# One layer of a hybrid diffusion backbone on one core: the first norm's modulation steps in one sequence, full-tile rotary parts, an early start on an operand

## The chip, the cores and the metric

The kernel runs on one core of one Trainium2 chip. A core has five engines, each with a queue of its own that it works through in order: TensorE (PE in the profile; its weight loads PEld), VectorE (DVE), ScalarE (ACT), GpSimd (POOL) and SyncE (SP), which here only issues DMAs. An instruction waits at the head of its queue until what it needs is there, and everything behind it waits too. The metric is the device time of one execution in microseconds (us).

## The reference

One layer is applied to 128 context tokens and 512 latent tokens, 640 in all, of width 2048. Context and latent tokens have conditioning vectors of their own.

```python
shift1, scale1, gate1, shift2, scale2, gate2 = split(silu(cond) @ w_ada + b_ada, 6)   # w_ada 2048 x 12288
h = rms_norm(x, g1) * (1 + scale1) + shift1
qkv, z, a, b, q_a, kv_a, k_pe = split(h @ w_in)
gdn_o = gated_deltanet(conv(qkv), z, a, b)              # 8 heads, both directions
q = rms_norm(q_a) @ w_q_b;  k, v = expand(rms_norm(kv_a) @ w_kv_b)
mla_o = softmax(([q_nope, rope(q_rope)] @ [k_nope, rope(k_pe)].T) * 192 ** -0.5) @ v   # 8 heads, rotary width 64
x = x + gate1 * (concat(gdn_o, mla_o) @ w_out)
h2 = rms_norm(x, g2) * (1 + scale2) + shift2
x = x + gate2 * conv_ffn(h2);  y = rms_norm(x, gf)
```

All is fp32. The kernel makes an fp32 product from three products of a faster format: a high part (a cast, on ACT) and a low part (operand minus high part, mostly on VectorE) of each operand, hi x hi + hi x lo + lo x hi.

## The kernel before

Tokens lie along the free axis: an operand tile is 128 features x 640 tokens, and a dense matmul covers 320 tokens. `dense` makes two output tiles (a pair) over four groups of four k-tiles (`kg`); `w_next` splits a weight chunk of 512 KB into its parts (`split_chunk`, lines 129 and 131) and loads further chunks ahead. A list scheduler of the framework fixes each engine's order from the program, so instructions of neighbouring steps interleave; which order results is seen in the program itself.

**First stage.** x is loaded in eight DMAs; ACT squares the sixteen k-tiles, VectorE adds them (line 381), and two fp32 matmuls with a matrix of ones give the column sums (line 244). A *modulation step* `ada(n, ...)` computes 256 columns of the modulation: four raw chunks of `w_ada` (`araw`, three buffers), each split (three buffers for the parts), 32 matmuls with four stationary columns (lines 264 and 265), a copy, and a closing product (line 272, four records in the trace). `part(j)`, for j = 0 to 7, does step j of scale1, makes the two modulated k-tiles (`modulated`: `h_hi` on ACT, `h_lo` on VectorE for even, on GpSimd for odd tiles, line 290), and the first three output tiles (z0 to z2) take them up. Then `dense` makes z3 and z4, with six modulation steps for shift1 (`NSP = 6`) put between its k-groups. The remaining four tiles of shift1 come from the *filler*, `gemv_fill`: VectorE multiplies raw rows of `w_ada` by the conditioning and adds up (lines 324 and 326, two instructions in each step of the filler), and a finish on TensorE (line 309, 16 small fp32 matmuls) closes a job of 16 steps. The shift's own product with `w_in` enters as two more columns (640 and 641) of `h`; z0 to z4 ran without them and get theirs by the filler later.

**Middle stage.** The other columns of `w_in`, with eight DeltaNet heads beside them; the filler goes on with gate1, shift2 and scale2.

**Attention.** 24 steps (8 heads x 3), each with scores, softmax, transposes and the product with v, and the projections of the next head pair in between. A score group is five products (line 1083); the rotary low part `qrl` has 64 rows, the other operands 128. `krs` holds the rotary key's high part in rows 0 to 63 and its low part in rows 64 to 127, `qrs` the query's high part twice. The filler ticks four times in each step by `FM = 0.25`.

**Output projection.** Eight pairs. `m_split(kg)` loads and splits the 16 operand tiles from `mix_d` in the first pair; the sinks add the residual (line 1195) and sum the squares (lines 1202 and 1203); the filler runs at one step for each tick, and what is left of it runs after the last pair. Then come the column sums (line 244) and the second norm.

Of the kernel before, what the change touches and what calls it, by code (L numbers as in the profile page):

```python
# [41 lines left out]
FM = 0.25  # L42
# [3 lines left out]
NSP = 6  # L46
LA = 1
# [3 lines left out]
PK = ()  # L51
SH = 1.0
# [15 lines left out]
def step_kernel(ctx: ExitStack, tc: tile.TileContext, a, dbg=None, stop=None):  # L68
# [183 lines left out]
    def ada_load(c, kg, pl):  # L252
        raw = pl.tile([P, 4, 256], F32, tag="wraw", name="araw", bufs=3)
        sp.dma_start(raw, a["w_ada"][c, kg])
        return raw

    def ada(n, t0, cond, pl):

        ps = bank("ada_ps")
        for kg in range(4):  # L260
            hi, lo = split_chunk(ada_load(n, kg, pl), 256, pl, 3, (4 * n + kg) % 8 in PK)
            for k in range(4):
                kt = kg * 4 + k
                pe.matmul(ps[0:4, 0:256], cond[:, kt, :], hi[:, k, :], start=kt == 0, stop=False)
                pe.matmul(ps[0:4, 0:256], cond[:, kt, :], lo[:, k, :], start=False, stop=kt == 15)
# [3 lines left out]
        def last():  # L269
            ps2 = bank("ada_ps2")  # L270
            for j in range(2):
                pe.matmul(ps2[:, 2 * j:2 * j + 2], m4[:, j * P:(j + 1) * P], con[0:4, K_COMB:K_COMB + 2],
                          start=True, stop=True)
            dve.tensor_tensor(mod[:, t0:t0 + 2, :], ps2[:, 0:4].rearrange("p (j c) -> p j c", c=2),
                              v1(V_BADA + t0, 2).unsqueeze(2).broadcast_to([P, 2, 2]), ALU.add)
# [7 lines left out]

    def modulated(x, rb, hi, lo, kt, scale, v):

        for cc, sl in ((0, slice(0, TL)), (1, slice(TL, T))):
            dve.scalar_tensor_tensor(v[:, sl], x[:, kt, sl], mod[:, scale + kt, cc:cc + 1], rb[:, sl],
                                     ALU.mult, ALU.mult)
        act.copy(hi[:, kt, 0:T], v)  # L289
        (pool if kt % 2 else dve).tensor_tensor(lo[:, kt, 0:T], v, hi.bitcast(F32)[:, kt, 0:T], ALU.subtract)  # L290
# [68 lines left out]
    h_hi = hp.tile([P, KT, T + 2], F32R, name="h_hi")  # L359
    h_lo = hp.tile([P, KT, T + 2], F32R, name="h_lo")  # L360
    zb = hp.tile([P, EZ, 2], F32, name="zb")

    def hmov(kt):
        return h_hi[:, kt, :], h_lo[:, kt, :]

    fill["ps"] = lambda: bank("ada_ps")
    with tc.tile_pool(name="xp", bufs=1, side="right") as xp:
        cond = xp.tile([P, KT, 4], F32R, name="cond")
        dve.tensor_copy(cond[:, :, 0:2], csil)
        dve.tensor_tensor(cond[:, :, 2:4], csil, cond.bitcast(F32)[:, :, 0:2], ALU.subtract)  # L370
        xs = xp.tile([P, KT, T], F32, name="xs")
        for c in range(8):
            sp.dma_start(xs[:, 2 * c:2 * c + 2, :], a["x"][:, 2 * c:2 * c + 2, :])
        acc = xp.tile([P, T], F32, name="acc1")
        for kt in range(KT):
            if kt == 0:
                act.activation(acc, xs[:, 0, :], AF.Square)
            else:
                sq = xp.tile([P, T], F32, tag="sq", name="sq", bufs=2)
                act.activation(sq, xs[:, kt, :], AF.Square)  # L380
                dve.tensor_tensor(acc, acc, sq, ALU.add)
        rb = xp.tile([P, T], F32, name="rb1")
        rstd_bcast(rb, col_sums(acc), 1.0 / D)

        def part(j):
            if j < 8:
                ada(j, 16 + 2 * j, cond, xp)()
                gain(16 + 2 * j, V_N1 + 2 * j, 2)
                for kt in (2 * j, 2 * j + 1):
                    v = xp.tile([P, T], F32, tag="sq", name="v", bufs=2)  # L390
                    modulated(xs, rb, h_hi, h_lo, kt, 16, v)

        def early(i, ps):

            zr = xp.tile([P, T], F32, tag="sq", name="zr", bufs=2)
# [1546 lines left out]
```

## Time and profile before

| | |
|---|---|
| median of 3 runs | 3266.69 us (3266.14 to 3268.99) |
| profiled execution | 3265.16 us, its span 3263.4 us |
| mean granted TensorE clock | 0.968 |
| TensorE, VectorE, ACT, GpSimd busy | 94%, 82%, 45%, 10% of the span |
| DMA | 403.92 MB, mean 124 GB/s |

Busy time of TensorE counts overlapping matmuls from the first start to the last end, so the distance of starts tells more of a matmul's price than its own duration. The granted clock is the share of 2.4 GHz that TensorE got; half is the lower of its two levels.

### The profile page before, as it was taken

The page shows a single profiled execution, that of the slowest core. Times are in us where ns is not written, and L with a number is a line of the kernel's source. Part 1 is how long each engine was busy: PE and PEld are TensorE (multiplying, and loading weights), DVE is VectorE, ACT ScalarE, POOL GpSimd, SP SyncE. Part 2 cuts the span into 40 slices and gives each one's busy share as a digit, 9 for nine tenths or more (in the row PEclk, how much of TensorE's full clock was granted, in tenths as well). Part 3 has the DMA queues.
Part 4 walks back from the last instruction along what each step waited for, and adds up shares of the span by engine and source line. Part 5 has one row for each costly group of instructions (what it writes and reads, how often), then busy time and mean ns, then how long its engine had stood idle before and what let it go on. Part 6 is the DMA issues. An engine that isn't in the chain of part 4 may idle for free. (4 is left out here: it accounts for less than half of the span.)

```text
span 3263.4 us, 54513 instructions
## 1 busy us (share of the span) xinstructions
PE 3071.6 (94%) x21243; PEld 2972.8 (91%) x21243; DVE 2684.3 (82%) x4701; ACT 1453.0 (45%) x2245; POOL 334.3 (10%) x279
## 2 busy tenths in 40 slices
PE   5899999999998998997899999999999989999996
PEld 4689999999998998997899999999999989999995
DVE  7666666767567677998998898898898898999998
ACT  5434555555446543114544444444444454444433
POOL 1201000000000000003200000000010041111111
PEclk9899999999899999998999999999999999999998
DMA  7663222323224126883343333343343332333333
GB/s 271 201 198 86 72 78 67 117 68 100 74 87 135 45 81 236 270 263 121 127 136 97 110 128 108 111 131 110 98 140 102 95 125 94 113 98 110 110 116 121
DMA packets 181474, 403.92 MB, mean 124 GB/s; under 512 B 39392, under 2 KB 57952, under 8 KB 181216
## 3 DMA queue, kind: packets, MB, share of 16 engines
q1 hardware_dynamic: 181216, 400.44, 38.3%
q8 instruction: 167, 2.74, 0.4%
q14 instruction: 91, 0.75, 0.1%
HBM read 361.83 MB, written 38.54 MB: 123 GB/s over the span
## 5 line engine op out<-in xcount | busy, mean ns | idle before, releaser
L922 ACT CAST whi<-wraw 128x1024 fp32r<-128x1024 f32 x256 | 268.8, 1050 | 489.4 <-PE dn L198 202.8
L198 PE MATMUL mm<-b_hi,whi 128*128 128x320 f32 x1344 | 398.6, 310 | 4.2 <-ACT whi L922 3.9
L198 PE MATMUL mm<-b_lo,whi 128*128 128x320 f32 x1344 | 397.8, 310 | 0.0
L923 DVE TENSOR_TENSOR wlo<-wraw,whi 128x1024 fp32r<-128x1024 f32 x256 | 318.0, 1242 | 71.9 <-PE dn L207 62.9
L326 DVE SCALAR_TENSOR_TENSOR aacc<-araw,csil,aacc 128x512 f32<-128x512 f32 x510 | 369.0, 762 | 9.1 <-DMA araw<-in_w_ada_dram 8.7
L198 PE MATMUL mm<-h_lo,whi 128*128 128x320 f32 (+1 forms) x1312 | 318.7, 321 | 17.5 <-POOL h_lo L290 17.5
L198 PE MATMUL mm<-h_hi,whi 128*128 128x320 f32 (+1 forms) x1312 | 324.2, 327 | 7.5 <-ACT h_hi L289 4.8
L198 PE MATMUL dn<-b_hi,whi 128*128 128x320 f32 x1008 | 297.7, 309 | 0.0
L198 PE MATMUL dn<-b_lo,whi 128*128 128x320 f32 x1008 | 297.7, 309 | 0.0
L129 ACT CAST whi<-wraw 128x1024 fp32r<-128x1024 f32 (+1 forms) x138 | 143.0, 1036 | 327.3 <-PE mm L198 227.1
L198 PEld LDWEIGHTS mm<-b_hi,whi 128*128 128x128 f32 x1344 | 253.2, 188 | 5.0 <-ACT whi L922 4.4
L198 PEld LDWEIGHTS mm<-b_lo,whi 128*128 128x128 f32 x1344 | 253.2, 188 | 0.0
L198 PEld LDWEIGHTS mm<-h_lo,whi 128*128 128x128 f32 x1312 | 227.3, 194 | 21.5 <-POOL h_lo L290 19.6
L198 PEld LDWEIGHTS mm<-h_hi,whi 128*128 128x128 f32 x1312 | 227.2, 195 | 13.0 <-ACT h_hi L289 6.8
L1593 PE MATMUL mm<-b_hi,whi 128*128 128x320 f32 x672 | 204.6, 318 | 33.1 <-DVE x_lo L1600 9.4
L207 PE MATMUL mm<-h_hi,wlo 128*128 128x320 f32 (+1 forms) x1312 | 234.1, 318 | 0.0
L922 ACT CAST whi<-us 128x1024 fp32r<-128x1024 f32 (+1 forms) x126 | 123.4, 980 | 230.7 <-PE mm L198 160.3
L207 PE MATMUL mm<-b_hi,wlo 128*128 128x320 f32 x1344 | 224.4, 309 | 0.0
L131 DVE TENSOR_TENSOR wlo<-wraw,whi 128x1024 fp32r<-128x1024 f32 (+1 forms) x138 | 168.2, 1219 | 54.2 <-ACT whi L129 23.7
L207 PEld LDWEIGHTS mm<-h_hi,wlo 128*128 128x128 f32 x1312 | 202.8, 192 | 1.6
L207 PEld LDWEIGHTS mm<-b_hi,wlo 128*128 128x128 f32 x1344 | 204.0, 188 | 0.0
L1593 PE MATMUL mm<-b_lo,whi 128*128 128x320 f32 x672 | 202.2, 314 | 0.0
(534 smaller groups left out, 7461.2 us busy)
## 6 DMA issues: line engine op xcount, KB each, us to landing
wraw<-in_w_up_dram SPq DMA_DIRECT2D x176, 512.0 KB
araw<-in_w_ada_dram SPq DMA_DIRECT2D x272, 256.0 KB
wraw<-in_w_down_dram SPq DMA_DIRECT2D x88, 512.0 KB
wraw<-in_w_in_dram SPq DMA_DIRECT2D x80, 512.0 KB
araw<-in_w_ada_dram SPq DMA_DIRECT2D x56, 512.0 KB
wraw<-in_w_out_dram SPq DMA_DIRECT2D x32, 512.0 KB
graw<-g_d SPq DMA_DIRECT2D x44, 320.0 KB
g_d<-cg SPq DMA_DIRECT2D x44, 256.0 KB
```

What stands on the lines that cost most here:

```text
L129: act.copy(hi[:, :, 0:n], raw[:, :, 0:n])
L131: (pool if on_pool else dve).tensor_tensor(lo[:, :, 0:n], raw[:, :, 0:n], hi.bitcast(F32)[:, :, 0:n], ALU.subtract)
L198: pe.matmul(o, wts[0][:, k, col:col + P], m[:, sl], start=start and k + n == 0, stop=False)
L207: pe.matmul(o, wts[1][:, k, col:col + P], mov(k)[0][:, sl], start=False, stop=stop and k == 3)
L326: dve.scalar_tensor_tensor(acc[:, c, 0:w], raw, vecs[:, kt, c:c + 1], acc[:, c, 0:w], ALU.mult, ALU.add)
L922: act.copy(dst_hi, src)
L923: dve.tensor_tensor(dst_lo, src, dst_hi.bitcast(F32), ALU.subtract)
L1593: pe.matmul(dq[q], wt(w[0], k), bs[(2 * n + k) % 6][m][:, q, :], start=n == grp[0] and k + m == 0, stop=False)
```

## The change

In the first stage:
- All 16 modulation steps (eight of scale1, eight of shift1, `NSP = 8`) run one after the other through `ada_next`; the closing product of a step and what hangs on it (`ada_last`) come after the next step's matmuls. The filler no longer runs here.
- There are eight raw buffers (`AR`) and five for each part (`AH`). In steps 0 to 7 the first of the four chunks isn't split: it goes into fp32 matmuls with an fp32 stationary operand (`condf`, whose columns 2 and 3 are zero).
- The squares of odd k-tiles go to TensorE (two fp32 matmuls each, of 320 columns), those of even ones are added on VectorE as before.
- x and `h` are eight tiles of two k-tiles, and a tile of `h_hi` takes the place of the x tile that it was made from. Both low parts of a step are on VectorE.

In attention and after it:
- `qrl` has 128 rows: ACT copies rows 0 to 63 into rows 64 to 127, and the product goes with the whole of `krs`.
- `FM` is 0.5: the filler gets twice as many ticks.
- In steps 19 to 22 the first four operand tiles of the output projection are loaded and split (`m_early`) into the room of `qn`, whose pool now lasts to the end of the projection.
- `neg` (minus the decay) is made for each head as `cc[:, 3]`.

```diff
-FM = 0.25
+FM = 0.5
-NSP = 6
+NSP = 8
+AR = 8
+AH = 5
     def ada(n, t0, cond, pl):
         ps = bank("ada_ps")
         for kg in range(4):
-            hi, lo = split_chunk(ada_load(n, kg, pl), 256, pl, 3, (4 * n + kg) % 8 in PK)
+            raw = pl.tile([P, 4, 256], F32, tag="wraw", name="araw", bufs=AR)
+            sp.dma_start(raw, a["w_ada"][n, kg])
+            whole = n < 8 and kg == 0
+            movs = ((1, raw),) if whole else [(0, w) for w in split_chunk(raw, 256, pl, AH)]
             for k in range(4):
                 kt = kg * 4 + k
-                pe.matmul(ps[0:4, 0:256], cond[:, kt, :], hi[:, k, :], start=kt == 0, stop=False)
-                pe.matmul(ps[0:4, 0:256], cond[:, kt, :], lo[:, k, :], start=False, stop=kt == 15)
+                for m, (c, w) in enumerate(movs):
+                    pe.matmul(ps[0:4, 0:256], cond[c][:, kt, :], w[:, k, :], start=kt + m == 0,
+                              stop=kt == 15 and m == 1)
...
-        (pool if kt % 2 else dve).tensor_tensor(lo[:, kt, 0:T], v, hi.bitcast(F32)[:, kt, 0:T], ALU.subtract)
...
         for kt in range(KT):
...
+            sq = acc if kt == 0 else xp.tile([P, T], F32, tag="sq", name="sq", bufs=4)
+            act.activation(sq, xs[kt // 2][:, kt % 2, 0:T], AF.Square)
+            if kt % 2:
+                for o, sl in tok_chunks(sums):
+                    pe.matmul(o, ones, sq[:, sl], start=kt == 1, stop=False)
+            elif kt:
                 dve.tensor_tensor(acc, acc, sq, ALU.add)
+        for o, sl in tok_chunks(sums):
+            pe.matmul(o, ones, acc[:, sl], start=False, stop=True)
...
+                    for k, v in enumerate(vs_):
+                        act.copy(h_hi[n][:, k, 0:T], v)
+                        dve.tensor_tensor(h_lo[n][:, k, 0:T], v, h_hi[n].bitcast(F32)[:, k, 0:T], ALU.subtract)
...
+        def ada_next(count):
+            for _ in range(count):
+                n = nada[0]
+                nada[0] += 1
+                f = ada(n, 16 + 2 * n if n < 8 else 2 * n - 16, (cond, condf), xp)
+                ada_last()
+                last.append((n, f))
...
         for kg in range(4):
-            for j in range(LA) if kg == 0 else ():
-                part(j)
-            for j in (2 * kg, 2 * kg + 1):
-                part(j + LA)
+            if kg == 0:
+                ada_next(1)
+                w_load(0)
+                w_load(1)
+            ada_next(3 if kg == 0 else 2)
...
-            ql = mp.tile([64, T], F32R, name="qrl", bufs=5)
+            ql = mp.tile([P, T], F32R, name="qrl", bufs=5)
...
-            dve.tensor_tensor(ql, rr[s, :], st_.bitcast(F32)[s, :], ALU.subtract)
+            dve.tensor_tensor(ql[0:64, :], rr[s, :], st_.bitcast(F32)[s, :], ALU.subtract)
+            act.copy(ql[64:128, :], ql.bitcast(F32)[0:64, :])
...
-                                    (qrl[:, qs], krs[0:64, :]))):
+                                    (qrl[:, qs], krs))):
...
+    def m_early(k):
+        if k == 0:
+            m_first.extend(qp.tile([P, 4, T], F32R, tag=f"qn_{q}", name=f"mf_{q}") for q in ("hi", "lo"))
+        raw = mp.tile([P, T], F32, tag="m0", name="m0", bufs=2)
+        sp.dma_start(raw, mix_d[k])
+        split(m_first[0][:, k, :], m_first[1][:, k, :], raw)
...
     for n, (h, x) in enumerate(steps):
+        if n in (19, 20, 21, 22):
+            m_early(n - 19)
```

SP's queue at the start of the program, from the first modulation weight on, before (`wraw` is a chunk of `w_in`, line 302 a row of the filler):

```order
L254 DMA araw<-in_w_ada_dram 128x1024 x3
L125 DMA wraw<-in_w_in_dram 128x1024
L254 DMA araw<-in_w_ada_dram 128x1024 x3
L125 DMA wraw<-in_w_in_dram 128x4x128
L125 DMA wraw<-in_w_in_dram 128x1024
L254 DMA araw<-in_w_ada_dram 128x1024 x3
L125 DMA wraw<-in_w_in_dram 128x4x128
L302 DMA araw<-in_w_ada_dram 128x512
L254 DMA araw<-in_w_ada_dram 128x1024 x3
```

and after:

```order
L257 DMA araw<-in_w_ada_dram 128x1024 x4
L125 DMA wraw<-in_w_in_dram 128x1024
L125 DMA wraw<-in_w_in_dram 128x4x128
L257 DMA araw<-in_w_ada_dram 128x1024 x12
L125 DMA wraw<-in_w_in_dram 128x1024
L125 DMA wraw<-in_w_in_dram 128x4x128
L257 DMA araw<-in_w_ada_dram 128x1024 x7
L125 DMA wraw<-in_w_in_dram 128x1024
L257 DMA araw<-in_w_ada_dram 128x1024
```

Sixteen raw chunks stand ahead of the second pair of `w_in` chunks, without a filler load among them, where three chunks stood ahead of the first.

VectorE at the start, from its sums of squares on, before (`wlo` are low parts of weights, `v` the modulated tile, `h_lo` its low part):

```order
L381 TENSOR_TENSOR acc_108<-acc_108,sq 128x640 x15
L131 TENSOR_TENSOR wlo<-araw,whi 128x1024 x3
L131 TENSOR_TENSOR wlo<-wraw,whi 128x1024
L131 TENSOR_TENSOR wlo<-araw,whi 128x1024 x3
L274 TENSOR_TENSOR mod<-ada_ps_223,vec 128x4
L131 TENSOR_TENSOR wlo<-wraw,whi 128x4x128
L282 SCALAR_TENSOR_TENSOR mod<-mod,vec 128x4
L287 SCALAR_TENSOR_TENSOR v<-xs,mod,rb_155 128x512
L287 SCALAR_TENSOR_TENSOR v<-xs,mod,rb_155 128x128
L287 SCALAR_TENSOR_TENSOR v<-xs,mod,rb_155 128x512
L287 SCALAR_TENSOR_TENSOR v<-xs,mod,rb_155 128x128
L131 TENSOR_TENSOR wlo<-araw,whi 128x1024
```

and after:

```order
L378 TENSOR_TENSOR acc_116<-acc_116,sq 128x640 x7
L131 TENSOR_TENSOR wlo<-araw,whi 128x1024 x3
L131 TENSOR_TENSOR wlo<-wraw,whi 128x1024
L131 TENSOR_TENSOR wlo<-wraw,whi 128x4x128
L273 TENSOR_TENSOR mod<-ada_ps,vec 128x4
L131 TENSOR_TENSOR wlo<-araw,whi 128x1024
L281 SCALAR_TENSOR_TENSOR mod<-mod,vec 128x4
L396 SCALAR_TENSOR_TENSOR v<-xs_90,mod,rb_174 128x512
L131 TENSOR_TENSOR wlo<-araw,whi 128x1024
L396 SCALAR_TENSOR_TENSOR v<-xs_90,mod,rb_174 128x128
L131 TENSOR_TENSOR wlo<-araw,whi 128x1024
L396 SCALAR_TENSOR_TENSOR v<-xs_90,mod,rb_174 128x512
```

Seven additions stand where fifteen stood, and the low parts of the second step's weights now lie between the parts of the first modulated tile.

VectorE at the end of the output projection, before (`aacc` is the filler, `xt` the residual in a sink, `acc` the sum of squares, `x2t` the second norm's operand):

```order
L326 SCALAR_TENSOR_TENSOR aacc<-araw,csil,aacc 128x512 x4
L1195 SCALAR_TENSOR_TENSOR xt<-pj,mod,xt 128x512
L1195 SCALAR_TENSOR_TENSOR xt<-pj,mod,xt 128x128
L326 SCALAR_TENSOR_TENSOR aacc<-araw,csil,aacc 128x512 x2
L1203 TENSOR_TENSOR acc_12702<-acc_12702,sq_15211 128x640
L326 SCALAR_TENSOR_TENSOR aacc<-araw,csil,aacc 128x512 x2
L1195 SCALAR_TENSOR_TENSOR xt<-mm_14949,mod,xt 128x512
L1195 SCALAR_TENSOR_TENSOR xt<-mm_14949,mod,xt 128x128
L326 SCALAR_TENSOR_TENSOR aacc<-araw,csil,aacc 128x512 x2
L1203 TENSOR_TENSOR acc_12702<-acc_12702,sq_15245 128x640
L326 SCALAR_TENSOR_TENSOR aacc<-araw,csil,aacc 128x512 x2
L131 TENSOR_TENSOR wlo<-wraw,whi 128x1024
```

and after:

```order
L337 TENSOR_TENSOR mod<-ada_ps,vec 128x8
L131 TENSOR_TENSOR wlo<-wraw,whi 128x1024
L281 SCALAR_TENSOR_TENSOR mod<-mod,vec 128x8
L131 TENSOR_TENSOR wlo<-wraw,whi 128x1024
L1222 SCALAR_TENSOR_TENSOR xt<-pj,mod,xt 128x512
L1222 SCALAR_TENSOR_TENSOR xt<-pj,mod,xt 128x128
L1230 TENSOR_TENSOR acc_12845<-acc_12845,sq_15274 128x640
L1222 SCALAR_TENSOR_TENSOR xt<-mm_15063,mod,xt 128x512
L1222 SCALAR_TENSOR_TENSOR xt<-mm_15063,mod,xt 128x128
L131 TENSOR_TENSOR wlo<-wraw,whi 128x1024
L1230 TENSOR_TENSOR acc_12845<-acc_12845,sq_15304 128x640
L1354 TENSOR_TENSOR x2t<-x2t,rb_15343 128x640 x4
```

The filler's rows no longer stand between and behind the last two sinks; its last output (`mod`) lies ahead of them.

## Rows read from the trace of the kernel before

**Rows 1.** Page, line 1: busy us, share and instructions of each engine.
```profile
PE 3071.6 (94%) x21243; PEld 2972.8 (91%) x21243; DVE 2684.3 (82%) x4701; ACT 1453.0 (45%) x2245; POOL 334.3 (10%) x279
```

**Rows 2.** Busy us by window; columns as the windows view prints them.
```profile
25.00:150.00 125.00, 97.91 (x604) 77.83 (x604) 95.20 (x125) 61.16 (x75) 30.97 (x8) 0.89 0.66 214
150.00:206.00 56.00, 54.03 (x399) 45.02 (x396) 35.56 (x39) 28.41 (x33) 0.00 (x0) 1.00 0.70 233
```

**Rows 3.** Waits of the first stage: us in total, times, longest.
```profile
ACT whi L129 <- DMA araw<-in_w_ada_dram: 25.7, 20, 2.5
PE mm L198 <- POOL h_lo L290: 17.5, 7, 4.3
```

**Rows 4.** Tile h_lo, who writes it: duration ns, least, median, most.
```profile
L290 POOL TENSOR_TENSOR h_lo<-v,h_hi x8: 1944/3907/6162, 39.2 to 136.2; 128x640 fp32r<-128x640 f32 x8
L290 DVE TENSOR_TENSOR h_lo<-v,h_hi x8: 814/818/821, 39.4 to 135.3; 128x640 fp32r<-128x640 f32 x8
```

**Rows 5.** Tile z_d, the stores into it: first and last start.
```profile
L397 SPq DMA_DIRECT2D z_d<-zr x5: 320/327/327, 143.4 to 205.7; - x5
```

**Rows 6.** Busy us by window in attention; last, the filler on VectorE.
```profile
1140.00:1180.00 40.00, 39.88 (x286) 37.30 (x285) 36.08 (x69) 16.72 (x37) 0.00 (x0) 1.00 0.42 127
1180.00:1243.00 63.00, 59.19 (x398) 51.19 (x396) 37.72 (x90) 28.52 (x69) 0.00 (x0) 1.00 0.09 33
...
1040.00:1243.00 203.00, 19.89 (x28) 1.00 0.18 58
```

**Rows 7.** Timeline around 1250: start, us, instruction, idle time before it.
```profile
1250.33 1.17 PE L198 MATMUL mm<-m_hi,whi 128*128 128x320 f32 x3 [7.93 <-ACT m_hi L922]
...
1255.88 0.59 PE L198 MATMUL mm<-m_hi,whi 128*128 128x320 f32 x2
...
1249.55 3.08 ACT L922 CAST m_hi<-m 128x640 fp32r<-128x640 f32 x4 [6.86 <-DMA m<-mix_d]
```

**Rows 8.** Timeline after the output projection: PE, then DVE and ACT.
```profile
1503.47 1.40 PE L244 MATMUL mm<-acc,con 128*128 128x320 f32 x2 [9.88 <-DVE acc L1203]
1504.67 3.41 PE L309 MATMUL ada_ps<-con,aacc 128*128 128x1 f32 x16
...
1500.28 0.99 DVE L1195 SCALAR_TENSOR_TENSOR xt<-mm,mod,xt 128x512 f32<-128x512 f32 x2
...
1501.30 0.74 ACT L1202 ACTIVATE sq<-xt 128x640 f32<-128x640 f32 x1 [3.56 <-DVE xt L1195]
```

**Rows 9.** Timeline of PE in the first stage, and tile qs_ps.
```profile
148.49 0.28 PE L264 MATMUL ada_ps<-whi,cond 128*4 128x256 f32 x1
...
151.12 0.28 PE L265 MATMUL ada_ps<-wlo,cond 128*4 128x256 f32 x1
...
154.02 0.60 PE L272 MATMUL ada_ps<-con,m 4*128 4x2 f32 x4
...
172.23 2.52 PE L207 MATMUL mm<-h_hi,wlo 128*128 128x320 f32 x16
174.58 0.28 PE L264 MATMUL ada_ps<-whi,cond 128*4 128x256 f32 x1
...
24.00 2.50 PE L244 MATMUL mm<-acc,con 128*128 128x320 f32 x4 [24.00 <-DVE acc L381]
...
L739 PE MATMUL qs_ps<-Sh,kq x64: 379/380/484, 376.7 to 979.4; 128*128 128x256 f32 x64
```

**Rows 10.** Busy us by window, for the last two columns, DMA.
```profile
180.00:200.00 20.00, 19.27 (x142) 15.71 (x141) 11.48 (x13) 9.32 (x12) 0.00 (x0) 1.00 0.68 221
1260.00:1280.00 20.00, 19.47 (x136) 19.20 (x136) 20.00 (x31) 7.42 (x10) 0.00 (x0) 1.00 0.99 350
```

**Rows 11.** Timeline of PE in a score group and behind it.
```profile
1228.23 0.46 PE L1083 MATMUL mm<-krs,qrs 128*128 128x320 f32 x2
1228.61 0.56 PE L1083 MATMUL mm<-krs,qrl 64*128 64x320 f32 x2
1229.10 0.44 PE L1134 MATMUL pt_ps<-con,pr 128*128 128x128 f32 x2
```

More of the change, by code (lines that the diff above doesn't have):

```diff
@@ L357, in step_kernel @@
     hp = hst.enter_context(tc.tile_pool(name="hp", bufs=1))
-    h_hi = hp.tile([P, KT, T + 2], F32R, name="h_hi")
-    h_lo = hp.tile([P, KT, T + 2], F32R, name="h_lo")
+    xs = [hp.tile([P, 2, HW], F32, name=f"xs{j}", tag=f"h_hi{j}") for j in range(8)]
+    h_hi, h_lo = [], []
     zb = hp.tile([P, EZ, 2], F32, name="zb")
     def hmov(kt):
-        return h_hi[:, kt, :], h_lo[:, kt, :]
+        return h_hi[kt // 2][:, kt % 2, :], h_lo[kt // 2][:, kt % 2, :]
     fill["ps"] = lambda: bank("ada_ps")
@@ L374, in step_kernel @@
         acc = xp.tile([P, T], F32, name="acc1")
+        sums = ps_pair(0)
         for kt in range(KT):
[L376 to L380, printed above, removed]
+            sq = acc if kt == 0 else xp.tile([P, T], F32, tag="sq", name="sq", bufs=4)
[4 more added lines that the diff above has]
+            elif kt:
@@ L381, in step_kernel @@
                 dve.tensor_tensor(acc, acc, sq, ALU.add)
+        for o, sl in tok_chunks(sums):
+            pe.matmul(o, ones, acc[:, sl], start=False, stop=True)
         rb = xp.tile([P, T], F32, name="rb1")
[L383 to L391, printed above, removed]
+        rstd_bcast(rb, sums[:, C0:C0 + T], 1.0 / D)
@@ new lines, in step_kernel, with ada_last @@
+        nada, last = [0], []
+        def ada_last():
+            if last:
+                n, f = last.pop()
+                f()
+                if n < 8:
+                    gain(16 + 2 * n, V_N1 + 2 * n, 2)
+                    vs_ = [xp.tile([P, T], F32, tag="sq", name="v", bufs=4) for _ in range(2)]
+                    for k, v in enumerate(vs_):
+                        for cc, sl in ((0, slice(0, TL)), (1, slice(TL, T))):
+                            dve.scalar_tensor_tensor(v[:, sl], xs[n][:, k, sl], mod[:, 16 + 2 * n + k, cc:cc + 1],
+                                                     rb[:, sl], ALU.mult, ALU.mult)
+                    h_hi.append(hp.tile([P, 2, HW], F32R, name=f"h_hi{n}", tag=f"h_hi{n}"))
+                    h_lo.append(hp.tile([P, 2, HW], F32R, name=f"h_lo{n}"))
+                    for k, v in enumerate(vs_):
+                        act.copy(h_hi[n][:, k, 0:T], v)
+                        dve.tensor_tensor(h_lo[n][:, k, 0:T], v, h_hi[n].bitcast(F32)[:, k, 0:T], ALU.subtract)
+                else:
+                    j, m = n - 8, mod[:, 2 * n - 16:2 * n - 14, :]
+                    act.copy(h_hi[j][:, :, T:T + 2], m)
+                    dve.tensor_tensor(h_lo[j][:, :, T:T + 2], m, h_hi[j].bitcast(F32)[:, :, T:T + 2], ALU.subtract)
@@ L417, in step_kernel @@
         bank_pool[0] = sst.enter_context(tc.tile_pool(name="pss2", bufs=4, space=PSUM))
-        fill["step"] = SH
-        fill["gen"] = gemv_fill([xp, 2, 1], ada_jobs(2 * NSP, 16))
-        todo = list(range(NSP))
-        last = []
         npair = (EZ - 3) // 2
@@ L580, in gdn @@
         dve.reciprocal(rec, ss)
[L581 removed]
+        cc = gp.tile([P, 4, 2, 5], F32, name="cc", bufs=2)
         for d in range(2):
@@ L1243, in o_sink @@
                 x_load(t + 4)
-            dense(lambda kt: (m_hi[:, kt, :], m_lo[:, kt, :]), o_sink, before=m_split if p == 0 else None, alloc=three)
+            dense(lambda kt: tuple(m[:, kt, :] for m in m_first) if kt < 4 else (m_hi[:, kt - 4, :], m_lo[:, kt - 4, :]), o_sink, before=m_split if p == 0 else None, alloc=three)
         for _ in fill["gen"]:
@@ L1249, in step_kernel @@
     nst.close()
+    qst.close()
     fst.close()
```

68 lines of the change are left out of this document (25 added, 43 removed).

## The prediction

> **What bounds the kernel now.** I read the page first: TensorE is busy 94% of the span, VectorE 82%, ACT 45% [rows 1]. So a change pays where it takes instructions from TensorE, where TensorE now waits, or where it runs at the lower of its two clock levels (1.2 instead of 2.4 GHz). Next come the stretches that the change touches. In the first stage (0 to 206 us) TensorE is busy 98 of 125 us between 25 and 150, at a granted clock of 0.89; from 150 on, 54 of 56 at 1.00 [rows 2]. The list of waits of that stage tells what ends last there: ACT waits 20 times for a modulation weight's DMA, 25.7 us in all, and TensorE 17.5 us for GpSimd's low parts of the normed operand [rows 3]. GpSimd takes 3.9 us for such a part where VectorE takes 0.82 [rows 4]. The stage ends with the last z store at 205.7 [rows 5]. In attention TensorE loses nothing between 1140 and 1180 and 4 of 63 us after that [rows 6]. It then stands idle 7.93 us before the output projection [rows 7], and 9.88 us after it, waiting for the sum of squares [rows 8].
>
> **The first stage: work.** Undisturbed, TensorE does a modulation matmul every 0.114 us (24 in a row from 148.49 to 151.12), a dense one every 0.147 us (16 from 172.23 to 174.58), and the four records that close a step in 0.60 us [rows 9]. Before, that is 448 x 0.114 + 480 x 0.147 + 14 x 0.60 = 51 + 71 + 8 = 130 us. From 25.8 to 205 it took 179, so 49 us (38%) went to waits and to the low clock. After, there are 16 steps and no filler on VectorE in this stage. The first quarter of steps 0 to 7 goes in as plain fp32: 32 such matmuls take the place of 64, and as the two new steps bring 64, 448 of the short kind stay. A 4x256 fp32 matmul does not occur before. The nearest row is the 128x256 fp32 product, two records of 0.38 us for each [rows 9]; a record of the short kind lasts 0.28 and comes every 0.114, so I take 0.38 - 0.17 = 0.21 us a record, 0.43 a matmul, 14 us for all. Bounds: 0.114 each (4 us), and 0.73 each (23 us) if they run as the fp32 sums at 24.00 did, two matmuls of 320 columns in 1.83 us, up to the next row at 25.83. With 16 x 0.60 the work is 51 + 71 + 14 + 10 = 146 us, 16 more than before.
>
> **The first stage: start.** The sums of squares move half to TensorE: 18 fp32 matmuls instead of 2. At the 0.92 us of that row they are 16.5 us from about 10 us on, beside ACT's sixteen squares, and end near 26, as before; at half that price ACT ends last, near 20. I count no gain. Then VectorE leads: up to the end of the second step it has six low parts of modulation weights, one and a half of dense weights and most of a modulated tile, some 10 us behind ACT's logarithm, exponential and casts, which end near 28. So the dense matmuls start near 38, when TensorE has done 12 of its 146 us; the other 134 would end at 172.
>
> **The first stage: losses.** What stood behind the two great waits is taken away: eight raw buffers instead of three let weights be asked for ahead, and no low part is left on GpSimd. VectorE, busy 95 of 125 us [rows 2], loses its filler and takes eight more operand parts (6.5 us). The weights are 64 x 0.52 + 5.2 = 39 MB. At the 350 GB/s that a full queue reaches at 1260 they need 111 us, from 17 to 128; at the 221 GB/s of 180 to 200, when three buffers held the queue, 176 us, to 193 [rows 10]. I take a loss of 8% of 134 us, between the 4% of 150 to 206 and the 38% of the whole stage, and get an end near 183: **22 us gained**. Bounds: no loss, 33 gained; 38% lost, 223, so 17 us given away.
>
> **Attention.** A score group's two matmuls on 64 rows take 0.49 us (1228.61 to 1229.10), and the two just ahead of them 0.38, where two of the ordinary dense kind take 0.29 [rows 9, 11]. The excess is 0.28 us, 32 times: 9 us. The Trainium skill, TensorE: Matmul & The Clock Gate, section "Why this matters for your kernels", says that a single matmul on 32 rows takes the time of one on 128; by it the full tile would save 0 and the sum would be 38. Against that, its page TensorEngine Tiling, "Key Properties", says that a change of tiling mode drains the engine, for which this trace has the 0.38 ahead of the group; so I go by the row. I take **8**, since from 1180 on TensorE is not full (59.2 of 63 us [rows 6]); bounds 0 and 13 (half as much again where a transpose stands between the two). The eight copies on ACT are hidden: it is busy 28.5 of the last 63 us; uncovered they would be 6 us.
>
> The filler in attention runs twice as often. Before it has 28 rows there and two openings, 15 steps [rows 6]; the new order has 32 steps. The 17 more, at two rows of 0.7 each, are 23 us of VectorE, besides 3 us for the four early tiles. At 1140 to 1180 VectorE was busy 36 of 40 us and TensorE lost nothing [rows 6]. But about half of the new rows fall in the last two heads, where no projection is left to fill TensorE. I charge **2**; bounds 0 and 11 (each of that half in the way of a softmax).
>
> **Output projection, start.** Its first four operand tiles are there, so the 7.93 us go, and with them the low clock: the first 20 matmuls took 5.55 us (1250.33 to 1255.88) for 20 x 0.147 = 2.9 [rows 7]. That is 10.5. What is late next are tiles 4 to 7: they are asked for at the same point as tiles 0 to 3 before, and cast from 1249.55 on, when the first 48 matmuls (7.1 us from 1242.4) end at 1249.5. About 1 us of wait, and some 2 for tiles 8 to 11, which stand behind six filler loads in SP's queue. **8 gained**; bounds 4 and 10.5.
>
> **Output projection, end.** The filler runs out during the last pair, as the new order shows. Then the last residual (0.99), its square (0.74) and its sum (0.8) follow the last matmul (1493.6) in some 3 us instead of 9.9, and the 3.4 us of closing matmuls leave the space between the two sums [rows 8]. **10 gained**; bounds 7 and 11.
>
> **Sum.** 22 + 8 - 2 + 8 + 10 = 46 us. The profiled execution took 3265.2 us, 1.5 less than the median of the runs shown; 3265.2 - 46 + 1.5 = 3221.
>
> **Rivals.**
> - *The first stage keeps its waits.* In-order queues only find new partners: VectorE for GpSimd, more work on TensorE. For it: 38% lost so far, and VectorE leads the first 38 us. Against: both great waits have a cause that goes. At 38% the stage costs 17 more, so the sum is 7 and the time 3260; at 22% (an end at 202) it gains 3, and the time is 3240.
> - *Attention gives it back.* The filler costs 11 and the full tile brings 0, as the softmax chain sets the pace: 46 - 9 - 8 = 29, 3238. For it: TensorE's 4 us lost from 1180 on. Against: none lost at 1140 to 1180. That 64 rows alone cost nothing would give 3229 (the page's rule above); the 0.49 speaks against it.
> - *The stage goes better.* Nothing lost and the upper ends elsewhere: 33 + 13 + 10.5 + 11 = 67, so 3199.
> - *Slower: the low clock in the first stage.* 64 modulation matmuls with four columns now stand in one row, and TensorE is fed in bursts before 38 us. At the low level 20 dense matmuls took 5.55 us [rows 7], 0.28 instead of 0.147 each, 0.9 us more for each us of work. All of the 134 us would cost 120, and the time 3341. It decides from 59 us on, when 65 of the 134 run low. Against: 24 short ones in a row kept 0.114 [rows 9], and the clock was 1.00 from 150 on.
>
> **How the numbers follow.** The forecast as summed has 0.60 (its own range 3206 to 3234), the first stage at 22% or more lost 0.15, attention giving back 0.08, the rule alone 0.03, the better case 0.08, the low clock 0.06. The range reaches from 3202 to 3248: it leaves out the best and the worst first stage and the low clock, some 0.2. What a measurement of this kernel tells from no change is about 0.2%, 6.5 us; the low clock, and the worst first stage with another loss beside it, are what ends nearer than that or beyond: faster 0.87, same 0.06, slower 0.07.
>
> **What would show it.** The last z store near 183 instead of 205.7, no TensorE wait on GpSimd, ACT's waits for weights well under 25 us; score matmuls of one spacing, 0.29 for each two; the output projection's first matmul within 1 us of attention's last; the sums some 3 us after its last matmul. The forecast is wrong if VectorE or a cast's buffer takes the place of the two waits in the first stage, if the granted clock before 150 stays under 0.9, or if TensorE idles in attention beside filler rows.

## The result and the profile after

The changed kernel takes 3233.65 us (median of four runs, 3224.20 to 3235.11) beside 3267.64 of the kernel before; the ratio is 0.989, 95% interval 0.987 to 0.9909. The profiled execution is the one of 3235.11 us, with a span of 3233.3; it is 30 us shorter than the profiled one of before, and the medians are 34 apart. Forecast were 46 and 3221, with a range of 3202 to 3248. So the sign and the range held, and some 12 us of the gain are missing. Where they are is best read from checkpoints: the start of an instruction that both programs have at the same place (first and last start in the lines of a tile).

| Checkpoint, us | before | changed | ahead by |
|---|---|---|---|
| last z store | 205.7 | 183.4 | 22.3 |
| last mix store of the recurrent heads | 1005.4 | 986.0 | 19.4 |
| first matmul on a rotary low part (scores) | 1040.4 | 1024.4 | 16.0 |
| last matmul on a rotary low part | 1232.7 | 1217.1 | 15.6 |
| last matmul of the output projection | 1493.3 | 1474.2 | 19.1 |
| column sums behind it | 1503.5 | 1477.6 | 25.9 |
| end of the span | 3263.4 | 3233.3 | 30.1 |

The first stage gave what was forecast. Attention, forecast as a gain of 6, lost 3.8 (its start 3.4, the scores 0.4). The output projection gave 3.5 up to its last matmul where 8 were forecast, and 11 behind that (6.8 before the sums, 4.2 after). Some 3 us went in the stretch of the recurrent heads, which the change hardly touches.

The busy line of the page, to be held against [rows 1], shows nothing of this: VectorE and ACT are as busy as before, and GpSimd lost 33 us.

```profile
PE 3075.9 (95%) x21331; PEld 2976.8 (92%) x21331; DVE 2652.0 (82%) x4692; ACT 1457.3 (45%) x2263; POOL 301.7 (9%) x272
```

The windows of the first stage do (for [rows 2]; columns as there): after the first 25 us shown, TensorE is full in every window and its granted clock is 1.00. What is lost now is lost before 50 us.

```profile
25.00:50.00 25.00, 20.11 (x103) 9.79 (x101) 16.23 (x23) 14.46 (x18) 0.00 (x0) 0.80 0.91 322
50.00:75.00 25.00, 25.00 (x168) 18.18 (x167) 20.30 (x31) 13.74 (x19) 0.00 (x0) 1.00 0.65 223
75.00:100.00 25.00, 25.00 (x176) 20.09 (x174) 21.37 (x33) 16.12 (x21) 0.00 (x0) 1.00 0.82 308
100.00:125.00 25.00, 25.00 (x184) 22.59 (x183) 19.77 (x27) 14.73 (x20) 0.00 (x0) 1.00 0.83 294
125.00:150.00 25.00, 25.00 (x195) 20.61 (x195) 18.09 (x22) 17.67 (x24) 0.00 (x0) 1.00 0.90 316
```

The two waits of [rows 3] are gone: in the list of waits of this stage TensorE has none for GpSimd, and ACT's for modulation weights, 25.7 us before, is this line (total, times, longest):

```profile
ACT whi L129 <- DMA araw<-in_w_ada_dram: 1.4, 2, 1.1
```

At the start of attention ACT's timeline shows the new copies (L1033, 0.73 us each) between the casts that were there:

```profile
1003.27 0.73 ACT L1033 CAST qrl<-qrl 64x640 fp32r<-64x640 f32 x1
...
1005.70 0.73 ACT L1033 CAST qrl<-qrl 64x640 fp32r<-64x640 f32 x1
...
1013.79 0.73 ACT L1033 CAST qrl<-qrl 64x640 fp32r<-64x640 f32 x1
1014.52 0.62 ACT L989 COPY sw<-kraw 32x512 f32<-32x512 f32 x1
1015.16 0.73 ACT L1033 CAST qrl<-qrl 64x640 fp32r<-64x640 f32 x1
1015.89 0.62 ACT L990 COPY sw<-kraw 32x512 f32<-32x512 f32 x1
1016.53 0.59 ACT L937 CAST vh<-mm 128x512 fp32r<-128x512 f32 x1
```

Two of them stand ahead of the copies for the rotary key (sw) and of the cast vh. VectorE makes vl from vh, the first score matmul waits for vl, and TensorE comes out of that wait at half speed (score pairs 0.53 us apart, weight-and-value matmuls 0.21 apart instead of 0.12). Its timeline there, the wait in the brackets:

```profile
1017.90 0.90 PE L1099 MATMUL mm<-kh,qh 128*128 128x320 f32 x2 [2.25 <-DVE vl L938]
1018.60 0.73 PE L1099 MATMUL mm<-kl,qh 128*128 128x320 f32 x2
1019.13 0.73 PE L1099 MATMUL mm<-kh,ql 128*128 128x320 f32 x2
1019.67 0.41 PE L1062 MATMUL pj<-whi,kv_hi 128*128 128x256 f32 x1
```

A score group has the spacing that was forecast, to be held against [rows 11]: 0.30 and 0.29 us from each pair to the next.

```profile
1215.12 0.45 PE L1099 MATMUL mm<-krs,qrs 128*128 128x320 f32 x2
1215.42 0.46 PE L1099 MATMUL mm<-krs,qrl 128*128 128x320 f32 x2
1215.71 0.71 PE L1150 MATMUL pt_ps<-con,pr 128*128 128x128 f32 x5
```

The output projection now begins at 1222.78, inside attention's last head, and not 7.93 us after its end [rows 7]. Behind it stand three new waits, and a second spell of half speed after the last of them:

```profile
1222.78 0.54 PE L198 MATMUL mm<-mf_hi,whi 128*128 128x320 f32 x2
...
1237.59 0.86 PE L198 MATMUL mm<-m_hi,whi 128*128 128x320 f32 x4 [2.05 <-ACT m_hi L937]
...
1247.03 0.85 PE L198 MATMUL mm<-m_hi,whi 128*128 128x320 f32 x4 [1.87 <-ACT m_hi L937]
1249.61 0.66 PE L198 MATMUL mm<-m_lo,whi 128*128 128x320 f32 x2 [1.72 <-DVE m_lo L938]
1250.06 0.74 PE L198 MATMUL mm<-m_hi,whi 128*128 128x320 f32 x2
1250.60 1.27 PE L198 MATMUL mm<-m_lo,whi 128*128 128x320 f32 x4
```

The end of the projection came as forecast, 3.06 us of wait where [rows 8] had 9.88, and no closing matmuls of the filler between the two sums:

```profile
1473.17 1.34 PE L207 MATMUL mm<-m_hi,wlo 128*128 128x320 f32 x8
1477.57 1.45 PE L244 MATMUL mm<-acc,con 128*128 128x320 f32 x4 [3.06 <-DVE acc L1230]
```

### The profile page after: what moved, and what is told of

It reads as the page before. It is cut to its first block, busy times and chain, and to the rows that moved or that the text cites. A ratio compares the mean times of both kernels' runs of the same rounds, so it can differ in the third digit from the quotient of the medians.

```text
span 3233.3 us, 54651 instructions
## 1 busy us (share of the span) xinstructions
PE 3075.9 (95%) x21331; PEld 2976.8 (92%) x21331; DVE 2652.0 (82%) x4692; ACT 1457.3 (45%) x2263; POOL 301.7 (9%) x272
## 5 line engine op out<-in xcount | busy, mean ns | idle before, releaser
L317 DVE SCALAR_TENSOR_TENSOR aacc<-araw,csil,aacc 128x512 f32<-128x512 f32 x480 | 342.4, 749 | 12.4 <-DMA araw<-in_w_ada_dram 12.0
```

The source lines that it names most:

```text
L317: dve.scalar_tensor_tensor(acc[:, c, 0:w], raw, vecs[:, kt, c:c + 1], acc[:, c, 0:w], ALU.mult, ALU.add)
```

## The experiments

Single executions of one kernel lie up to 13 us from their median here, so an edit worth 3 us is read from its own stretch of the profile, by the checkpoints above, and the total only bears it out. "Scores" is the stretch between the first and the last matmul on a rotary low part; "start" the one before it, from the recurrent heads' last store; "projection" the one from the last such matmul to the output projection's last matmul. How far these stretches repeat is seen where an edit leaves them alone: in six profiles with the changed kernel's attention the scores took 192.4 to 192.7 us and the start 37.8 to 38.7; in nine profiles with four tiles made ahead the projection took 255.3 to 257.9.

**Filler rate of attention.**

```diff
-FM = 0.5
+FM = 0.25
```

> The changed kernel with the filler of attention back at half its rate (FM 0.25). Theory A, that the doubled filler on VectorE ate what the full rotary tile saved: from the first to the last score matmul some 185 us instead of 193.0, and the steps left over come back at the end of the output projection, where TensorE again waits 7 to 10 us for the sum of squares; in all 3230 to 3236. Rival B, that the softmax chain sets attention's pace and the filler is free there: the scores still take 193 us and only the end is lost, 3240 to 3244.

3242.81 us, 9 more than the changed kernel. The scores took 188.8 us instead of 192.7, so the doubled filler costs 3.9 in attention. But the steps left over come back at the end: TensorE waits 9.75 us for the sum of squares again, and the closing matmuls stand between the sums again.

```profile
1481.49 1.41 PE L244 MATMUL mm<-acc,con 128*128 128x320 f32 x2 [9.75 <-DVE acc L1230]
```

A is half right about the scores (188.8, not 185) and right about the wait at the end; the total is B's. The filler rate is a trade of 4 us in attention for 11 or 12 behind the projection (the table's 11.0, in this run 12.7), and the change makes it well.

**Zeros from GpSimd in place of ACT's copies.** The upper 64 rows of the low part meet the low part of the key; with zeros there the sum is that of the kernel before, on a full tile.

```diff
-            act.copy(ql[64:128, :], ql.bitcast(F32)[0:64, :])
+            pool.memset(ql[64:128, :].bitcast(F32), 0.0)
```

> The changed kernel, but the upper 64 rows of each rotary low part are set to zero by GpSimd instead of copied there by ACT; the product is then that of 64 rows, on a full tile. Theory A, that the four ACT copies at the start of attention (0.73 us each, 2.9 us together) lie on the chain to the first scores: the first score group starts 3 to 4 us sooner against the end of the projection before it, and the whole is 3 to 5 us shorter, 3229 to 3231. Rival B, that ACT's copies are hidden and the start is late for a DMA or for VectorE: no change, 3233.6 within 2. Rival C, that GpSimd's memset is late or in VectorE's way: slower by 1 to 5.

3225.98 us. The start took 36.4 us instead of 38.4 and the scores 188.2 instead of 192.7: 6.5 together. That is A's mechanism, but less at the start than A had (2.0, not 3 to 4) and more in all, for the four copies in the middle of attention count as well. GpSimd, otherwise idle there, makes five of the eight before the first is needed (988.44 to 991.4, VectorE's low part at 998.2):

```profile
988.44 2.92 POOL L1033 MEMSET qrl<- 64x640 f32 x5 [141.44 <-DVE qa L960]
```

**Rotary low parts back on 64 rows**, without copies.

```diff
-            ql = mp.tile([P, T], F32R, name="qrl", bufs=5)
+            ql = mp.tile([64, T], F32R, name="qrl", bufs=5)
...
-                                    (qrl[:, qs], krs))):
+                                    (qrl[:, qs], krs[0:64, :]))):
```

> The changed kernel with the rotary low parts back on 64 rows and without ACT's copies; the rest as changed. Theory A, that a matmul on 64 rows costs 0.28 us a score group on the chip and nothing hides it: from the first to the last score 201 us instead of 193.0, less 3.5 us at the start of attention, 3238 in all. Rival B, that attention from the first score on is paced by the softmax chain and the filler, and the full tile is worth nothing there: the scores take 193 to 195 us, and with the 3.5 us of the start the kernel is 1 to 3 us faster than the changed one, 3231.

3235.38 us, start 35.8, scores 198.3. Against the run with zeros, which differs from this one in the tile and in GpSimd's eight instructions alone, that is 10.1 us of scores: A's mechanism, a little above its price. Against the changed kernel it is 5.6 us of scores, between A and B because ACT's copies went as well, less 2.6 at the start, so 3 in all: the copies eat two thirds of what the tile gives. The rows show the price in the same program, 0.39 us ahead of the group of 64 rows and 0.48 for it:

```profile
1215.62 0.45 PE L1098 MATMUL mm<-krs,qrs 128*128 128x320 f32 x2
1216.01 0.56 PE L1098 MATMUL mm<-krs,qrl 64*128 64x320 f32 x2
1216.49 0.87 PE L1149 MATMUL pt_ps<-con,pr 128*128 128x128 f32 x6
```

**No operand tiles ahead.** The output projection loads and casts all sixteen after attention.

```diff
-        if n in (19, 20, 21, 22):
-            m_early(n - 19)
...
-        m_hi = op.tile([P, 12, T], F32R, name="m_hi")
+        m_hi = op.tile([P, KT, T], F32R, name="m_hi")
```

> The changed kernel without the four operand tiles made ahead: the output projection again loads and casts all sixteen tiles after attention. Theory A, that the tiles made ahead are worth the wait of 7.9 us and the low clock behind it, less the new waits for tiles 4 to 11 (2.05, 1.87 and 1.72 us): slower by 5 to 8, 3239 to 3242. Rival B, that the waits only move to the later tiles and the loads in attention cost as much: within 2 of 3233.6. Rival C, that what ends last in the output projection is VectorE's filler and residuals, so that a late start costs nothing: the column sums start at the same time, 3233.

3243.52 us (3234.66 to 3245.05). The projection stretch took 261.9 us, as before the change (260.6), against 257.1: 4.8 for the four tiles, just below A and far from B and C. Four profiles without tiles made ahead have 260.6 to 262.3, so this is clear of the scatter. Another 2.7 us are scores of 195.4 us, and those go with the clock: between 1075 and 1125 it was 0.90 and 0.93 in this run, where the changed kernel had 0.97 and 1.00 at the same place, with fewer matmul records in the same time.

```profile
1075.50:1100.50 25.00, 24.41 (x164) 23.70 (x163) 21.54 (x45) 11.48 (x25) 0.00 (x0) 0.90 0.35 103
1100.50:1125.50 25.00, 23.25 (x145) 22.74 (x143) 23.39 (x41) 21.38 (x37) 0.00 (x0) 0.93 0.32 103
```

What the tiles cost in attention is better read at the place where their casts and low parts stand, 1154.7 to 1163.4 in the changed kernel. The two score groups around it start at 1149.84 and 1170.22, 20.4 us apart; in the run without tiles the same two start at 1152.79 and 1172.56, 19.8 apart, both at a granted clock of 1.00. So the tiles cost 0.6 us there, and nothing at the start (38.6, against 38.4). First the changed kernel, then the run without tiles:

```profile
1149.80:1170.20 20.40, 19.75 (x135) 19.21 (x134) 11.03 (x22) 9.77 (x18) 0.00 (x0) 1.00 0.17 59
```

```profile
1152.70:1172.50 19.80, 19.56 (x134) 19.05 (x133) 8.15 (x18) 7.12 (x14) 0.00 (x0) 1.00 0.08 28
```

**The first stage alone**: the last three edits undone together (filler rate, 64 rows, no tiles ahead).

```diff
-FM = 0.5
+FM = 0.25
...
-            act.copy(ql[64:128, :], ql.bitcast(F32)[0:64, :])
...
-        if n in (19, 20, 21, 22):
-            m_early(n - 19)
```

> The changed kernel with attention and the output projection as before (filler at its old rate, rotary low parts on 64 rows, no tiles ahead), so that what is new is the first stage with its sixteen steps (and one small VectorE instruction more for each head of the next stage). Theory A, that the first stage alone is worth 22 us and keeps it to the end: last z store between 178 and 184, the scores take 192 us again, TensorE waits 10 us for the sums after the output projection, and the whole gains 20 to 26 us against the kernel before. Rival B, that the middle of the program gives some of it back for a reason that lies in the change: the time from the last z store to the last store of the recurrent heads is 803 or more where the kernel before has 799.7, and the gain is under 19 us.

3248.48 us, ratio 0.9933 (0.9916 to 0.995). Last z store 182.8, start 34.8, scores 192.2, projection 261.7, 10.2 us from its last matmul to the sums: the first stage keeps its 22 us to the end, and attention and projection are those of before. The stretch of the recurrent heads took 804.6, as B has it, but the gain, 20.7 us, is A's.

**No plain fp32 quarters.**

```diff
-            whole = n < 8 and kg == 0
+            whole = False
```

> The changed kernel with every modulation weight split into high and low parts, so without the plain fp32 quarters: 64 short matmuls for 32 fp32 ones. Theory A, that in the first 60 us VectorE leads and the fp32 quarters are there to relieve it: eight low parts more at 1.2 us, of which those of the first steps are on the chain, and the last z store comes 1 to 6 us later. Rival B, that TensorE alone sets the stage: 32 x 0.455 = 14.6 us of fp32 give way to 64 x 0.114 = 7.3, and the last z store comes 7 us sooner.

3225.56 us, last z store at 175.1. In seven profiles of the changed first stage it lies between 178.5 and 183.8, 181.8 in the mean, so B is right: 3 to 9 us gained, where it had 7. The total owes something to luck besides: in this profile (an execution of 3217.41 us) the stretch of the recurrent heads, which the edit leaves alone, took 794.0 us, the shortest of all. VectorE was busier (107.6 us between 25 and 150 instead of 95.8), and TensorE no emptier (120.5 instead of 120.1). The fp32 quarters had cost what was forecast; the changed kernel's timeline has four such matmuls (eight records) in 1.82 us, 0.455 each where 0.43 were taken:

```profile
51.44 1.89 PE L264 MATMUL ada_ps<-araw,condf 128*4 128x256 f32 x8
53.26 0.28 PE L264 MATMUL ada_ps<-whi,cond 128*4 128x256 f32 x1
```

**Which of the two great waits was worth the 22 us?** Four kernels: the changed one with three raw buffers; with the odd low parts of the operand on GpSimd; with both; and the kernel before with its low parts on VectorE.

```diff
-AR = 8
+AR = 3
```

> The changed kernel with three raw buffers for modulation weights instead of eight. Theory A, that ACT's 25.7 us of waiting for these weights had the three buffers for a cause: the wait comes back, and the last z store is 8 to 15 us later than 178 to 184. Rival B, that the weights came late before for the other work of the stage (GpSimd's low parts held the operand, and with it everything behind): the last z store stays within 3 us.

```diff
-                        dve.tensor_tensor(h_lo[n][:, k, 0:T], v, h_hi[n].bitcast(F32)[:, k, 0:T], ALU.subtract)
+                        (pool if k else dve).tensor_tensor(h_lo[n][:, k, 0:T], v, h_hi[n].bitcast(F32)[:, k, 0:T], ALU.subtract)
```

> The changed kernel with the odd low parts of the normed operand back on GpSimd, eight at 3.9 us. Theory A, that they held TensorE: it waits for them again, and the last z store is 8 to 15 us later than 178 to 184. Rival B, that with weights asked for ahead TensorE has other work while GpSimd makes its part, and VectorE, which leads, is relieved of 8 x 0.82 us: within 3 us, or sooner.

> The changed kernel with both causes back in its new order: three raw buffers and the odd low parts on GpSimd. Theory A, that GpSimd's parts cost only where the weights come late: the last z store well behind the 191.3 of three buffers alone, 197 to 205. Rival B, that the order of the steps is what made GpSimd's parts harmless: 190 to 193, and the 12 to 14 us that are still missing to 205.7 belong to the order and to the filler.

And of the kernel before:

```diff
-        (pool if kt % 2 else dve).tensor_tensor(lo[:, kt, 0:T], v, hi.bitcast(F32)[:, kt, 0:T], ALU.subtract)
+        dve.tensor_tensor(lo[:, kt, 0:T], v, hi.bitcast(F32)[:, kt, 0:T], ALU.subtract)
```

> The kernel before with all low parts of the normed operand on VectorE, so that only GpSimd's part in its first stage is undone. Theory A, that TensorE's 17.5 us of waiting for GpSimd were lost time: the last z store comes 8 to 15 us sooner than 205.7. Rival B, that behind that wait stands the one for the weights (three raw buffers), and TensorE only waits for another engine: within 4 us of 205.7.

(The totals of the kernel before and of the changed one are those of the first comparison; beside the edited kernels the kernel before took 3266.82 and 3269.19.)

| First stage | weights | odd low parts | last z store | total, us |
|---|---|---|---|---|
| before | 3 buffers | GpSimd | 205.7 | 3267.64 |
| before, edited | 3 buffers | VectorE | 188.0 | 3250.86 |
| changed | 3 buffers | GpSimd | 196.0 | 3246.24 |
| changed | 3 buffers | VectorE | 191.3 | 3241.86 |
| changed | 8 buffers | GpSimd | 181.2 | 3232.91 |
| changed | 8 buffers | VectorE | 178.5 to 183.8 | 3233.65 |

In the old order the low parts alone are worth 17.7 us. In the new order they are worth 4.7 with three buffers (between A's and B's numbers) and nothing with eight (181.2, where the seven profiles of the changed first stage have 181.8 in the mean). The buffers are worth 8 to 13 us, or 15 with the low parts on GpSimd. So A holds for the three buffers, B for the low parts in the new order, and in the old order A, with more than it had. The two waits are not two terms of a sum. That GpSimd costs so little in the new order doesn't hang on the eight buffers. TensorE waits 0.9 us for it with eight and 1.0 with three, against 17.5 before [rows 3]; with three the line is:

```profile
PE mm L198 <- POOL h_lo L402: 1.0, 1, 1.0
```

So the rest of the first stage's change, the order of the steps and the filler's end, took this wait away, and with eight buffers the low parts could have stayed on GpSimd. Moving them helped in the old order although ACT's wait for weights then rose from the 25.7 of [rows 3]:

```profile
ACT whi L129 <- DMA araw<-in_w_ada_dram: 39.9, 31, 4.1
```

and with three buffers in the new order that wait is longer still, 38 times and 51.0 us:

```profile
ACT whi L129 <- DMA araw<-in_w_ada_dram: 51.0, 38, 4.3
```

The stage of the edited kernel before ends only 4 to 10 us after the changed one's, but does fourteen steps, not sixteen. What is left between 196.0 and 205.7, with both causes back, is the order, the filler, the sums on TensorE, the fp32 quarters and the five buffers for the parts; no run takes these apart. The eight buffers alone in the kernel before were not tried, so what they would give in the old order stays open. Apart from the changed first stage each row of the table is a single profile.

**A better version.** Four edits together: zeros from GpSimd, no fp32 quarters, FM = 0.4375, and eight operand tiles ahead, the second four in the buffers of the keys' and values' operand (kv_hi, kv_lo), free by then.

```diff
-FM = 0.5
+FM = 0.4375
...
-            act.copy(ql[64:128, :], ql.bitcast(F32)[0:64, :])
+            pool.memset(ql[64:128, :].bitcast(F32), 0.0)
...
-            whole = n < 8 and kg == 0
+            whole = False
...
-    kv_hi = m1.tile([P, 4, 768], F32R, name="kv_hi")
+    kv_hi = qp.tile([P, 4, 768], F32R, tag="kv_hi", name="kv_hi")
...
         if n in (19, 20, 21, 22):
-            m_early(n - 19)
+            m_early(2 * n - 38)
+            m_early(2 * n - 37)
```

> The changed kernel with four edits together, each read from its own stretch: no fp32 quarters (last z store near 175 instead of 178 to 184); zeros from GpSimd instead of ACT's copies and the filler of attention at 0.4375 instead of 0.5 (scores from 192.5 to some 185 to 187 us, TensorE's wait for the sums after the output projection still near 3); eight operand tiles of the output projection made ahead instead of four. Theory A, that what costs the output projection 2.05, 1.87 and 1.72 us is the late loads and casts of tiles 4 to 11: from the last score to its last matmul 250 to 253 us instead of 257. Rival B, that the four more tiles and their casts take as much from attention as they give: scores 190 or more. In all 3212 to 3220 by A, 3222 by B.

3222.16 us, ratio 0.9863 (0.985 to 0.9877): 45 us faster than before, and 14 faster than the changed kernel beside it (3236.26, below). Last z store 174.6, start 35.1, scores 190.4, projection 253.0, 3.4 us to the sums. One wait of 1.62 and one of 0.47 stand where three had stood, and two more, of 1.24 and 0.28, ahead of the filler's closing matmuls, which now fall into the projection (3.6 us in all, where it had 5.6):

```profile
1229.14 0.38 PE L300 MATMUL ada_ps<-con,aacc 128*128 128x1 f32 x2 [1.24 <-DVE aacc L317]
1233.47 1.43 PE L198 MATMUL mm<-m_hi,whi 128*128 128x320 f32 x4 [1.62 <-ACT m_hi L937]
1235.38 0.90 PE L198 MATMUL mm<-m_lo,whi 128*128 128x320 f32 x2 [0.47 <-DVE m_lo L938]
```

So A's mechanism holds for the projection (4 us), and the total is B's. The scores took 190.4 with less filler, where the run with zeros and four tiles had 188.2, so about half of the 4 us is net. That the four more tiles are what attention pays for is B's reading; with four edits at once no run shows it alone.

**The changed kernel once more.**

> The changed kernel itself once more, as a measure for the others of this call. If the differences of some us between its executions come from the granted clock, its last z store lies between 178 and 184, the stretch from there to the last store of the recurrent heads between 794 and 808, and the rest of its checkpoints within 1 us of the first profile of it: scores 192.7, from the last score to the output projection's last matmul 257.1.

3236.26 us (3232.59 to 3239.99). Last z store 182.9, scores 192.6, start 38.7; the projection 255.3, 1.8 under the first profile. The stretch of the recurrent heads took 810.4, a little above what was expected.

## Why the prediction was right, and where it was not

**First stage, +22: right in size, for a reason that is only half the one given.** The z store came at 183.4, forecast 183, and the price of the fp32 quarters, the fullness of TensorE and the end of both waits came as said. The argument "both great waits have a cause that goes" named the eight buffers and VectorE's low parts as the cure. With both of these undone the changed order still ends at 196.0, 9.7 us sooner than before, and without the wait for GpSimd. The buffers bring the rest; beside them the moved low parts bring nothing. The start was misjudged by 8 us (the first dense matmul at 46.4, not 38). This was made good by no idle time from 50 us on, where 8% of 134 us, 11, was charged for losses; that the two errors cancel is luck. The low clock, the rival that would have made the kernel slower, came only in spells before 46 us (from 39.3 on modulation matmuls stood 0.21 us apart, not 0.114): 0.80 from 25 to 50, then 1.00.

**Attention, +8 − 2: the step that failed.** The tile itself gives 10.1 us, so the row of 0.49 us was rightly taken. The Trainium skill says of a single matmul on 32 rows that it takes the time of one on 128 (TensorE: Matmul & The Clock Gate, "Why this matters for your kernels"). Carried over to the 64 rows here, this does not hold: the pair on 64 rows takes 0.48 us and costs the pair ahead of it 0.10, in a program that does full pairs in 0.29. The Trainium skill also states that a change of tiling mode drains TensorE (TensorEngine Tiling (Array Packing), "Key Properties"). The 0.10 may be that drain, but no run separates the two.

What failed is "the eight copies on ACT are hidden: it is busy 28.5 of the last 63 us". That window holds no copy. A copy follows the low part that it copies, and the trace of before has these low parts (tile `qrl`) between 1020.8 and 1133.0, the first four by 1033, where ACT was already busy 14.3 of 15 us:

```profile
L1017 DVE TENSOR_TENSOR qrl<-rr,qrs x8: 807/814/820, 1020.8 to 1133.0; 64x640 fp32r<-64x640 f32 x8
1020.00:1035.00 15.00, 13.58 (x93) 13.33 (x93) 13.42 (x19) 14.34 (x22) 0.00 (x0) 1.00 0.37 122
```

In the changed kernel four copies stand at the start of attention, where ACT is one chain of copies and casts with TensorE at its end, and four between 1108 and 1121, where ACT is busy 23.1 of 25 us, VectorE 23.5 and TensorE 22.6:

```profile
1099.40:1124.40 25.00, 22.59 (x148) 21.65 (x147) 23.54 (x40) 23.13 (x40) 0.00 (x0) 1.00 0.34 107
```

The text itself gave "uncovered they would be 6 us"; that is what they cost, 2.0 at the start and 4.5 in the scores, by the run with zeros. The filler was charged 2 and costs 3.9 on the full tile. Start and scores together show how the terms meet: 227.3 us before, 234.1 with the new filler rate and the early tiles on 64 rows (6.8 more), 224.6 with the full tile and zeros (9.5 less), 231.1 with ACT's copies (6.5 more). That is the loss of 3.8. Of the 6.8 the four tiles are 0.6 where they stand. That the filler costs more beside 64 rows than the 3.9 of the full tile would account for the rest, but no run shows it alone.

**Output projection, start, +8: half.** 4.8 by the run without early tiles. The forecast had two waits of 1 and 2 us; there are three, 5.6 us together, and the low clock after the third (0.72 between 1250 and 1256). The first, 2.05, is the forecast wait for tiles 4 to 7. For the second the cause was named (tiles 8 to 11 stand behind six filler loads in SP's queue) and undersized: they went out at 1239.78.

```profile
1233.34 1.75 SPq L1240 DMA_DIRECT2D m<-mix_d  x4
1235.14 0.43 SPq L1245 DMA_DIRECT2D xt<-in_x_dram  x1
1235.61 3.10 SPq L293 DMA_DIRECT2D araw<-in_w_ada_dram  x6
1239.78 3.30 SPq L1240 DMA_DIRECT2D m<-mix_d  x4
```

The third was not foreseen. The first high part of these tiles was in use at 1247.03, but VectorE still had ten filler rows ahead of the low parts:

```profile
1242.10 6.71 DVE L317 SCALAR_TENSOR_TENSOR aacc<-araw,csil,aacc 128x512 f32<-128x512 f32 x10 [0.78 <-DMA araw<-in_w_ada_dram]
1248.74 3.02 DVE L938 TENSOR_TENSOR m_lo<-m,m_hi 128x640 fp32r<-128x640 f32 x4
```

**Output projection, end, +10: right** (6.8 before the sums, 4.2 behind them), and by the reason given: the run with the old filler rate loses it again.

**Not in the sum: the recurrent heads.** 3 us less were ahead at their end than at their start. The stretch took 794.0 to 810.4 us in twelve profiles of the changed order there, 803.4 in the mean, and 799.7 and 800.1 in two of the old one. The instructions are the same in the twelve, and TensorE's busy time and granted clock move with it. The shortest and the longest (columns as in [rows 2]):

```profile
175.10:969.10 794.00, 758.68 (x5787) 724.09 (x5786) 541.82 (x1435) 397.16 (x776) 43.92 (x44) 0.96 0.30 93
```

```profile
182.90:993.30 810.40, 776.20 (x5786) 740.62 (x5786) 540.80 (x1435) 397.51 (x776) 44.95 (x44) 0.94 0.30 91
```

Whether 3 of these us belong to the change (two VectorE rows more for each head, 0.16 us each) can't be told from a scatter of 16, and stays open.

## What to carry to other kernels

Cover for an added instruction has to be read where the instruction will stand, not from a stretch of the same stage with room: here the copies went to the two places at which ACT was nearly full. Two waits in one stage need not be two terms of a sum: here the rest of the change took one of them away, and the cure meant for it could have been left out. And where a product needs a full tile, an idle engine's zeros serve as well as a busy engine's copy.

## What was not expected of the hardware

Executions of one program differ by more than some of the edits, and the granted clock goes with them: the nine of the changed kernel lie between 3224.20 us, at 0.975, and 3239.99, at 0.970. In two kernels that share the stretch of the recurrent heads, its 5786 or 5787 matmul records kept TensorE busy 758.7 us at 0.96 and 776.2 at 0.94. GpSimd, which takes 3.9 us for a subtraction of 128x640 here, sets 64x640 to zero in 0.63. And between 1250 and 1256 the DMA engines moved 387 GB/s, above the 350 that the prediction took for a full queue.
